# The four links of a head's norm get places of their own in an iteration of the attention loop

## The chip, the cores and the metric

One NeuronCore of a Trainium2 chip runs the whole program. The metric is the device time of one execution in microseconds (us). An execution is also recorded by the hardware profiler; its rows are quoted below. Engines: PE is TensorE (PEld its weight loads), DVE is VectorE, ACT is ScalarE, POOL is GpSimd, SP issues DMAs.

## The reference, cut to what matters

The program is two blocks of two layers each, on 256 positions of width 1024. The first block's layers hold the attention that the change touches. A layer of it attends with 4 heads; a head has two softmax maps, whose difference weighs the values, and each head's output is normalized over its 128 channels:

```python
def diff_attn(q, k, v, lam):
    s = jnp.einsum('bhqd,bhkd->bhqk', q, k).astype(jnp.float32) * (HEAD_DIM ** -0.5)
    a = jax.nn.softmax(s, axis=-1).reshape(b, N_HEADS, 2, nq, nk)
    w = a[:, :, 0] - lam * a[:, :, 1]
    return jnp.einsum('bhqk,bhkd->bhqd', w.astype(v.dtype), v)

def head_out(o, g_sub, lam_init):
    o = rms_norm(o, g_sub) * (1.0 - lam_init)
    b, h, n, d = o.shape
    return o.transpose(0, 2, 1, 3).reshape(b, n, h * d)
```

The 256 positions of `x` attend to 512 keys (256 of the context, 256 of their own). In the first layer the 256 context positions also attend, to their own 256 keys. Beside attention, a layer pools (`pool_mixer`), projects with `w_out` and runs an MLP; `ada_params` gives its shifts, scales and gates from `c @ w_ada`.

## The kernel before

Everything runs in float32. A weight matrix arrives in pieces of 512 rows (`raw`), is split into a high part (`whi`, ScalarE, L111) and the rest (`wlo`, VectorE, L119), and every product takes three passes: high by high, high by low, low by high. `Stream` holds this pipeline; a product takes a unit of weights at a time, and its `tick` and `next` put the splits of later units between the matmuls. Most matmuls are issued at L593.

Each engine runs its instructions in the order in which the program issues them, so the order of the lines is the schedule. Work that is to lie beside other work is written as generators, whose `next` runs one more piece: `fill(i)` gives `FILL[l][i]` pieces of the layer's other products (values' projection `v_gemm`, pooling's projection `u_gemm` with its windows L933 to L951, pooling's product L958 to L967, the first half of `w_out`), and `st.ada_step()` gives `STEPS[l][i]` pieces of the next layers' `ada_params`, whose weights come as `araw` (sums on VectorE at L278 and L280, or products on TensorE at L293, with a copy at L296, transposes at L301 and a sum at L303).

`attend` (L973) runs the attention of one layer. Its items are, for `x`, a head's first and second 128 queries (8 items), and in the first layer a context head's 256 queries (4 more). The loop has two iterations more than items. In iteration i:

- `scores(i + 1)` puts the next item's products on TensorE (L987);
- `soft(i)` runs its first piece: maxima (DVE, L997), their scaling (L998) and the exponentials (ACT, L1002);
- `before`, the third piece of `soft(i-1)`, is the weighted difference of the two maps (DVE, L1012);
- `fill(i)`;
- the second piece of `soft(i)`: reciprocal and scaling of the sums (DVE, L1006 and L1007), scaling of the second map (ACT, L1009);
- the adaLN steps;
- the rest of the norm of a head whose values were begun one iteration ago: the product with `ones` (PE, L1037), Ln and Exp (ACT, L1039 and L1040), the scaled output (DVE, L1041), and `split`, its high part (ACT, L445) and the rest (DVE, L446);
- `flip(i - 1)`: transposes of the weighted maps (PE, L1024) and their copy `wT` (ACT, L1025);
- two iterations after a head's last item, `values` begins: the products with the values (PE, L1033) and the squares of the result (ACT, L1035).

There are 12 heads in all: 4 of `x` and 4 of the context in the first layer, 4 of `x` in the second. In the first layer the heads of `x` begin in iterations 3, 5, 7 and 9, those of the context in 10 to 13; in the second layer the heads begin in iterations 3, 5, 7 and 9. The last head of each layer ends behind the loop.

Of the kernel before, what the change touches and what calls it, by code (L numbers as in the profile page):

```python
# [71 lines left out]
class Stream:  # L72
# [90 lines left out]
    def next(self, hold=False):  # L163
        u = self.cur
        self.cur += 1
        self.held = self.held + 1 if hold else 1
        self.split_to(self.cur)
        if self.HI_AT < 0:
            self.high_to(self.room())
        self.due += self.quota[u]  # L170
        return self.parts.pop(u)
# [8 lines left out]
def _body(es, tc, I, out, dbg, stop):  # L180
    nc = tc.nc
    mm, act, dve, pool_e, pe = nc.tensor.matmul, nc.scalar, nc.vector, nc.gpsimd, nc.tensor
# [8 lines left out]
    def bank(shape=(128, 2, T)):  # L191
        return ps.tile(list(shape), F32, tag="ps", bufs=8, name="ps")

    def scr(shape, tag="s", bufs=5, dt=F32):
        return (mp if tag in SMALL else sp).tile(list(shape), dt, tag=tag, bufs=bufs, name=tag)

    def scr1(shape=(128, T)):
        return scr(shape, tag="s1", bufs=6)
# [14 lines left out]
    def w4(name, shape):  # L213
        return sp.tile(list(shape), F32, tag="w4", bufs=2, name=name)
# [229 lines left out]
    def split(src, hi, lo, lo_eng=None):  # L444
        act.copy(hi, src)  # L445
        (lo_eng or dve).tensor_sub(lo, src, hi)  # L446
# [242 lines left out]
    def run(g):  # L689
        for _ in g:  # L690
            pass
# [135 lines left out]
    for k in range(8):  # L827
# [3 lines left out]
        for a in range(0, 0 if k in DIRECT else 4, 2):  # L831
            hi = wp.tile([128, 2, 512], F32R, tag="whi", bufs=Stream.BUFS, name="whi")
            lo = wp.tile([128, 2, 512], F32R, tag="wlo", bufs=Stream.BUFS, name="wlo")
# [26 lines left out]
    h = {}  # L860
# [112 lines left out]
    def attend(l, segs, qT, kT, v, operand, look, fill):  # L973

        items = [(s, h, qts) for s in segs for h in range(4) for qts in (((0,), (1,)) if s == 0 else ((0, 1),))]
        keys_of = {0: (0, 1, 2, 3), 1: (2, 3)}
        sc, wts, wT = {}, {}, {}

        def scores(i):
            if i >= len(items):  # L980
                return
            s, h, qts = items[i]
            nk, k0 = 128 * len(keys_of[s]), 128 * keys_of[s][0]
            sc[i] = [bank([128, len(qts), nk]) for _ in range(2)]
            for a, qt in enumerate(qts):
                for j in range(2):
                    mm(sc[i][j][:, a], qT[64 * j:64 * j + 64, h, s * T + qt * 128:s * T + qt * 128 + 128],  # L987
                       kT[64 * j:64 * j + 64, h, k0:k0 + nk], start=True, stop=True)

        def soft(i):  # L990
            s, _, qts = items[i]
            nq, nk = len(qts), 128 * len(keys_of[s])
            m = scr([128, 2, 2], tag="m2", bufs=3)[:, :, :nq]
            z = scr([128, 2, 2], tag="z2", bufs=3)[:, :, :nq]
            banks, e = sc.pop(i), []
            for j in range(2):
                dve.reduce_max(m[:, j], banks[j], axis=AX)  # L997
            dve.tensor_scalar(m, m, -0.125, None, op0=OP.mult)  # L998
            for j in range(2):
                ei = scr([128, nq, nk])  # L1000
                for a in range(nq):
                    act.activation(ei[:, a], banks[j][:, a], AF.Exp, bias=m[:, j, a:a + 1], scale=0.125,  # L1002
                                   accum_out=z[:, j, a:a + 1])
                e.append(ei)
            yield
            dve.reciprocal(z, z)  # L1006
            dve.tensor_mul(z[:, 1], z[:, 1], lam[l].to_broadcast([128, nq]))  # L1007
            for a in range(nq):
                act.activation(e[1][:, a], e[1][:, a], AF.Copy, scale=z[:, 1, a:a + 1])  # L1009
            yield  # L1010
            for a in range(nq):
                dve.scalar_tensor_tensor(e[0][:, a], e[0][:, a], z[:, 0, a:a + 1], e[1][:, a], op0=OP.mult, op1=OP.add)  # L1012
            wts[i] = e[0]

        def flip(i):
            s, h, qts = items[i]
            n = len(keys_of[s])
            w = wts.pop(i)
            if qts[0] == 0:
                wT[s, h] = w4("wT", [128, 4, T])  # L1020
            p = bank([128, n, len(qts), 128])
            for a in range(len(qts)):
                for j in range(n):
                    pe.transpose(p[:, j, a], w[:, a, j * 128:(j + 1) * 128], ident)  # L1024
            act.copy(wT[s, h][:, :n, qts[0] * 128:(qts[-1] + 1) * 128].rearrange("p n (a t) -> p n a t", t=128), p)  # L1025

        def values(s, h):
            t, keys = wT.pop((s, h)), keys_of[s]
            hi, lo = operand(s)
            b = bank()  # L1030
            p, p2 = b[:, 0], b[:, 1]
            for i, kt in enumerate(keys):
                mm(p, v[:, kt, h * 128:(h + 1) * 128], t[:, i], start=i == 0, stop=i == len(keys) - 1)  # L1033
            o = scr1()
            act.activation(o, p, AF.Square)  # L1035
            yield
            mm(p2, ones, o, start=True, stop=True)  # L1037
            r = scr1()
            act.activation(r, p2, AF.Ln, bias=eps, scale=1.0 / 128)  # L1039
            act.activation(r, r, AF.Exp, scale=-0.5)  # L1040
            dve.scalar_tensor_tensor(o, p, gsub[:, l:l + 1], r, op0=OP.mult, op1=OP.mult)  # L1041
            split(o, hi[:, 4 + h], lo[:, 4 + h])

        for i in range(look):
            scores(i)
        vals = None
        before = iter(())
        last = {(s, h): max(i for i, x in enumerate(items) if x[:2] == (s, h)) for s, h, _ in items}
        for i in range(len(items) + 2):
            scores(i + look)  # L1050
            now = soft(i) if i < len(items) else iter(())
            next(now, None)
            next(before, None)
            fill(i)
            next(now, None)
            for _ in range(STEPS[l][i]):
                st.ada_step()
            before = now
            if vals is not None:
                next(vals, None)  # L1060
                vals = None
            if 1 <= i <= len(items):
                flip(i - 1)
            for sh, at in last.items():
                if i == at + 2:
                    vals = values(*sh)
                    next(vals)
        if vals is not None:
            next(vals, None)

    def hooked(g, at, f):

# [108 lines left out]
    def first_layer(l, norm, h):  # L1181
# [155 lines left out]
        if l == 0:  # L1337
            small_setup()
        attend(l, segs, qT, kT, v, operand, 1, fill)
        mark("w_out")  # L1340
        st.ahead = st.BUFS
# [707 lines left out]
```

## Time and profile before

| | |
|---|---|
| time, median of 3 runs | 1658.03 us (1655.99 to 1660.52) |
| time of the profiled execution | 1653.65 us |
| its span in the profile | 1651.9 us |
| TensorE busy | 1571.6 us (95%) |
| VectorE busy | 1221.6 us (74%) |
| ScalarE busy | 862.8 us (52%) |
| GpSimd busy | 82.5 us (5%) |
| mean granted TensorE clock | 0.97 |

The profile's times are microseconds from the span's start. The attention loop of the first layer lies at about 105 to 237, that of the second at about 695 to 769. A row of the trace's order of time gives the start, the duration, the engine, the line, the operation, what it writes and reads, shapes, a count where like rows are merged, and in brackets the idle time of the engine before it with what ended it.

### The profile page before, as it was taken

How to read it: one execution, taken by the hardware profiler on the slowest of the kernel's cores; microseconds unless marked ns; L12 is line 12 of the kernel's file. 1: busy time of each engine (PE TensorE's matmuls, PEld its weight loads, DVE VectorE, ACT ScalarE, POOL GpSimd, SP SyncE). 2: the span in 40 equal slices, each digit the busy share in tenths (PEclk: the TensorE clock that was granted, in tenths of full speed). 3: DMA queues.
4: the chain of work that ended last, by engine and by line, in shares of the span. 5: the costliest groups of instructions: out<-in, count | busy, mean ns of one | idle time of the engine just before them, and what ended most of it. 6: DMA issues, size and time to landing. Idle time of an engine off the chain costs nothing.

```text
span 1651.9 us, 31245 instructions
## 1 busy us (share of the span) xinstructions
PE 1571.6 (95%) x12917; PEld 1475.2 (89%) x12917; DVE 1221.6 (74%) x2105; ACT 862.8 (52%) x1471; POOL 82.5 (5%) x202
## 2 busy tenths in 40 slices
PE   7899798999999999798999999989999999899998
PEld 2886488999999999777999998669999998899998
DVE  6885478899978777656856677568886788897673
ACT  5646356522222225765744457436664558766463
POOL 0010000112121120000000000000000000000000
PEclk9999999999999999998999999779999999999999
DMA  9353323355455553212656554115655544555551
GB/s 367 121 153 106 122 90 118 128 179 180 155 202 192 192 180 109 77 52 90 211 179 202 179 179 129 52 58 175 203 180 180 198 153 159 179 178 185 178 197 55
DMA packets 134014, 256.89 MB, mean 156 GB/s; under 512 B 6224, under 2 KB 19184, under 8 KB 132848
## 3 DMA queue, kind: packets, MB, share of 16 engines
q1 hardware_dynamic: 132672, 254.31, 46.4%
q8 instruction: 101, 1.65, 0.4%
q10 hardware_dynamic: 1200, 0.59, 0.1%
q14 instruction: 41, 0.34, 0.1%
HBM read 253.83 MB, written 1.05 MB: 154 GB/s over the span
## 4 chain that ended last, share of the span: by engine, by line
PE 81%; DVE 8%; ACT 8%; issue 2%; DMA 1%; SPq 0%; DVEq 0%; ACTq 0%
PE ps L593 73%; DVE wlo L119 2%; ACT whi L111 1%; PE ps L987 1%; ACT s L922 1%; ACT s L524 1%; PE ps L293 1%; PE ps L1033 1%; ACT s L1002 1%; DMA raw<-in_w_ada_dram 1%; DVE s L942 1%; PE ps L1610 1%; DVE X L714 0%; PE ps L1024 0%; PE ps L1684 0%
## 5 line engine op out<-in xcount | busy, mean ns | idle before, releaser
L111 ACT CAST whi<-raw 128x1024 fp32r<-128x1024 f32 x380 | 394.2, 1048 | 427.5 <-PE ps L593 392.1
L119 DVE TENSOR_TENSOR wlo<-raw,whi 128x1024 fp32r<-128x1024 f32 x380 | 459.1, 1221 | 160.9 <-ACT whi L111 155.9
L593 PE MATMUL ps<-hid,whi 128*128 128x256 f32 x2304 | 295.5, 283 | 0.0
L593 PEld LDWEIGHTS ps<-hid,whi 128*128 128x128 f32 x2304 | 284.8, 192 | 0.0
L593 PE MATMUL ps<-h2hi,whi 128*128 128x256 f32 x672 | 162.2, 283 | 4.9 <-ACT h2hi L525 4.9
L593 PE MATMUL ps<-h2lo,whi 128*128 128x256 f32 x672 | 161.9, 281 | 0.0
L593 PE MATMUL ps<-hid,wlo 128*128 128x256 f32 x1152 | 156.8, 283 | 0.0
L593 PE MATMUL ps<-fhi,whi 128*128 128x256 f32 x640 | 155.3, 281 | 0.0
L593 PE MATMUL ps<-flo,whi 128*128 128x256 f32 x640 | 155.3, 281 | 0.0
L280 DVE SCALAR_TENSOR_TENSOR aacc<-araw,cs,aacc 128x512 f32<-128x512 f32 x182 | 129.1, 747 | 25.5 <-DMA araw<-in_w_ada_dram 24.6
L593 PEld LDWEIGHTS ps<-hid,wlo 128*128 128x128 f32 x1152 | 146.4, 192 | 0.0
L593 PEld LDWEIGHTS ps<-h2hi,whi 128*128 128x128 f32 x672 | 128.1, 191 | 5.3 <-ACT h2hi L525 5.3
L593 PEld LDWEIGHTS ps<-h2lo,whi 128*128 128x128 f32 x672 | 127.5, 190 | 0.3 <-DVE h2lo L527 0.3
L593 PE MATMUL ps<-dhi,whi 128*128 128x256 f32 (+1 forms) x512 | 126.5, 285 | 0.0
L593 PE MATMUL ps<-dlo,whi 128*128 128x256 f32 (+1 forms) x512 | 124.9, 281 | 0.0
L593 PEld LDWEIGHTS ps<-fhi,whi 128*128 128x128 f32 x640 | 121.1, 189 | 0.0
L593 PEld LDWEIGHTS ps<-flo,whi 128*128 128x128 f32 x640 | 120.5, 188 | 0.0
L593 PEld LDWEIGHTS ps<-dhi,whi 128*128 128x128 f32 x512 | 96.9, 189 | 0.5 <-issue 0.3
L593 PEld LDWEIGHTS ps<-dlo,whi 128*128 128x128 f32 x512 | 97.0, 189 | 0.2
L714 DVE SCALAR_TENSOR_TENSOR X<-ps,ada,X 128x256 f32<-128x256 f32 x184 | 75.9, 476 | 20.1 <-PE ps L593 20.1
L593 PE MATMUL ps<-fhi,wlo 128*128 128x256 f32 x640 | 89.3, 282 | 0.0
L593 PE MATMUL ps<-h2hi,wlo 128*128 128x256 f32 x672 | 88.8, 281 | 0.0
(392 smaller groups left out, 2820.4 us busy)
## 6 DMA issues: line engine op xcount, KB each, us to landing
raw<-in_w_mlp_dram SPq DMA_DIRECT2D x64, 1024.0 KB, 5.5
raw<-in_ffn_w_up_dram SPq DMA_DIRECT2D x48, 1024.0 KB, 5.1
araw<-in_w_ada_dram SPq DMA_DIRECT2D x80, 512.0 KB, 4.0
raw<-in_ffn_w_down_dram SPq DMA_DIRECT2D x24, 1024.0 KB, 5.3
raw<-in_w_in_dram SPq DMA_DIRECT2D x16, 1024.0 KB, 5.6
raw<-in_ev_w_in_dram SPq DMA_DIRECT2D x12, 1024.0 KB, 5.0
raw<-in_w_out_dram SPq DMA_DIRECT2D x8, 1024.0 KB, 4.8
raw<-in_od_w_in_dram SPq DMA_DIRECT2D x8, 1024.0 KB
```

The lines of the kernel that those rows point to most:

```text
L111: self.nc.scalar.copy(hi, src)
L119: self.nc.vector.tensor_sub(lo, src, hi)
L280: dve.scalar_tensor_tensor(a[:, v], raw[:, k], c, a[:, v], op0=OP.mult, op1=OP.add)
L293: mm(p[:2], cs[:, :, 2 * q + k], raw[:, k], start=q == 0 and k == 0, stop=q == 3 and k == 1)
L524: act.activation(h, src, AF.Identity, bias=sa(n), scale=gs(n))
L593: mm(p, w, x, start=start, stop=stop, skip_group_check=True)
L714: dve.scalar_tensor_tensor(X[:, n, s], b[:, i], gates[s](n), X[:, n, s], op0=OP.mult, op1=OP.add)
L922: act.copy(sw[32 * q:32 * q + 32], src[32 * (q ^ 1):32 * (q ^ 1) + 32])
L942: dve.tensor_add(c[:, :, :width], a[:, :, :width], a[:, :, n:n + width])
L987: mm(sc[i][j][:, a], qT[64 * j:64 * j + 64, h, s * T + qt * 128:s * T + qt * 128 + 128], kT[64 * j:64 * j + 64, h, k0:k0 + nk], start=True ...
L1002: act.activation(ei[:, a], banks[j][:, a], AF.Exp, bias=m[:, j, a:a + 1], scale=0.125, accum_out=z[:, j, a:a + 1])
L1033: mm(p, v[:, kt, h * 128:(h + 1) * 128], t[:, i], start=i == 0, stop=i == len(keys) - 1)
```

## The change

The norm of a head now runs in five pieces instead of two, and the loop calls them at places of their own. `values` gets three more `yield`s, and `split` is written out as its two operations. In the loop, `vals` is the head that was begun in the iteration before, and `old` the head before that. At the top of an iteration, ahead of the next scores, comes the product with `ones`. Behind the second piece of `soft(i)` come Ln and Exp. Behind the adaLN steps come the scaled output and its high part. The rest (the low part) comes in the iteration after that, behind the third piece of `soft(i-1)` and ahead of `fill`. Behind the loop, `run` ends what is left of the last two heads.

```diff
@@ values
             mm(p2, ones, o, start=True, stop=True)
+            yield
             r = scr1()
             act.activation(r, p2, AF.Ln, bias=eps, scale=1.0 / 128)
             act.activation(r, r, AF.Exp, scale=-0.5)
+            yield
             dve.scalar_tensor_tensor(o, p, gsub[:, l:l + 1], r, op0=OP.mult, op1=OP.mult)
-            split(o, hi[:, 4 + h], lo[:, 4 + h])
+            act.copy(hi[:, 4 + h], o)
+            yield
+            dve.tensor_sub(lo[:, 4 + h], o, hi[:, 4 + h])
@@ the loop
-        vals = None
-        before = iter(())
+        vals = old = before = iter(())
         last = {(s, h): max(i for i, x in enumerate(items) if x[:2] == (s, h)) for s, h, _ in items}
         for i in range(len(items) + 2):
+            next(vals, None)
             scores(i + look)
             now = soft(i) if i < len(items) else iter(())
             next(now, None)
             next(before, None)
+            next(old, None)
             fill(i)
             next(now, None)
+            next(vals, None)
             for _ in range(STEPS[l][i]):
                 st.ada_step()
             before = now
-            if vals is not None:
-                next(vals, None)
-                vals = None
+            next(vals, None)
+            old, vals = vals, iter(())
             if 1 <= i <= len(items):
                 flip(i - 1)
             for sh, at in last.items():
                 if i == at + 2:
                     vals = values(*sh)
                     next(vals)
-        if vals is not None:
-            next(vals, None)
+        run(old)
+        run(vals)
```

## Rows read from the trace of the kernel before

**Rows 1.** The page: busy time by engine, and the chain that ended last.
```profile
PE 1571.6 (95%) x12917; PEld 1475.2 (89%) x12917; DVE 1221.6 (74%) x2105; ACT 862.8 (52%) x1471; POOL 82.5 (5%) x202
...
PE 81%; DVE 8%; ACT 8%; issue 2%; DMA 1%; SPq 0%; DVEq 0%; ACTq 0%
```
**Rows 2.** Busy time in two stretches: length, each engine, clock, DMA share, GB/s.
```profile
136.00:237.00 101.00, 88.39 (x494) 61.70 (x494) 53.31 (x123) 52.28 (x133) 0.00 (x0) 0.95 0.31 101
714.00:769.00 55.00, 45.00 (x281) 38.22 (x281) 30.88 (x80) 29.83 (x73) 0.00 (x0) 0.88 0.19 63
```
**Rows 3.** Line 1041, VectorE's idle time before it: releaser, us in total, times.
```profile
  ACT s L1040: 28.4, 10
```
**Rows 4.** Order of time, TensorE, first layer: its waits in the loop.
```profile
174.46 1.88 PE L293 MATMUL ps<-araw,cs 128*2 128x512 f32 x4 [2.13 <-DMA araw<-in_w_ada_dram]
...
187.25 2.23 PE L293 MATMUL ps<-araw,cs 128*2 128x512 f32 x3 [2.03 <-DVE ada L303]
...
204.88 0.58 PE L301 MATMUL ps<-ident,arow 2*128 2x2 f32 x4 [3.48 <-ACT arow L296]
...
213.85 0.38 PE L593 MATMUL ps<-mhi,whi 128*128 128x256 f32 x1 [1.64 <-ACT mhi L964]
...
236.45 0.70 PE L1037 MATMUL ps<-s,ones 128*128 128x256 f32 x2 [1.39 <-ACT s L1035]
```
**Rows 5.** Order of time, TensorE, second layer: values of two heads, and waits.
```profile
730.64 1.89 PE L1033 MATMUL ps<-wT,v 128*128 128x256 f32 x8
...
746.19 1.11 PE L1024 MATMUL ps<-ident,s 128*128 128x128 f32 x4 [4.88 <-DVE s L1012]
747.10 3.62 PE L1033 MATMUL ps<-wT,v 128*128 128x256 f32 x8
752.13 0.70 PE L958 MATMUL ps<-uT,wpool 128*128 128x256 f32 x2 [1.42 <-ACT uT L951]
756.03 1.22 PE L958 MATMUL ps<-uT,wpool 128*128 128x256 f32 x2 [3.19 <-ACT uT L951]
...
768.05 0.70 PE L1037 MATMUL ps<-s,ones 128*128 128x256 f32 x2 [0.47 <-ACT s L1035]
```
**Rows 6.** Order of time, TensorE, first layer: the values of three heads.
```profile
134.32 1.89 PE L1033 MATMUL ps<-wT,v 128*128 128x256 f32 x8
...
196.63 1.89 PE L1033 MATMUL ps<-wT,v 128*128 128x256 f32 x8
...
219.73 1.03 PE L1033 MATMUL ps<-wT,v 128*128 128x256 f32 x4
```
**Rows 7.** Order of time, ScalarE, first layer: the squares of the same heads.
```profile
137.81 0.39 ACT L1035 ACTIVATE s<-ps 128x256 f32<-128x256 f32 x1
...
200.75 0.38 ACT L1035 ACTIVATE s<-ps 128x256 f32<-128x256 f32 x1
...
225.65 0.39 ACT L1035 ACTIVATE s<-ps 128x256 f32<-128x256 f32 x1
```
**Rows 8.** Order of time, second layer: scaling of head 1, squares of heads 2 and 3.
```profile
723.88 0.48 DVE L1041 SCALAR_TENSOR_TENSOR s<-ps,gsub,s 128x256 f32<-128x256 f32 x1 [5.43 <-ACT s L1040]
...
737.43 0.40 ACT L1035 ACTIVATE s<-ps 128x256 f32<-128x256 f32 x1
...
759.20 0.39 ACT L1035 ACTIVATE s<-ps 128x256 f32<-128x256 f32 x1
```
**Rows 9.** Order of time, VectorE and ScalarE: the norm of the first context head.
```profile
224.35 0.48 DVE L1041 SCALAR_TENSOR_TENSOR s<-ps,gsub,s 128x256 f32<-128x256 f32 x1
225.30 0.43 DVE L446 TENSOR_TENSOR mlo<-s,mhi 128x256 fp32r<-128x256 f32 x1 [0.47 <-ACT mhi L445]
...
224.86 0.41 ACT L445 CAST mhi<-s 128x256 fp32r<-128x256 f32 x1 [3.69 <-DVE s L1041]
225.17 0.58 ACT L1025 COPY wT<-ps 128x512 f32<-128x512 f32 x1
```
**Rows 10.** Busy time in a stretch behind the 4.88 wait (columns as in rows 2).
```profile
746.00:748.00 2.00, 1.81 (x7) 1.63 (x8) 1.34 (x3) 2.00 (x6) 0.00 (x0) 0.50 0.00 0
```

## The prediction

> **What bounds the kernel now.** I read the page first: TensorE is busy 95% of the span and carries 81% of the chain that ended last [rows 1]. So a change can only matter where TensorE stands. The table of stretches comes next. It gives the two attention loops, from the values of the first head to the last product with `ones`: in the first layer's 101.0 us TensorE worked 88.4, in the second layer's 55.0 it worked 45.0, at a mean clock of 0.95 and 0.88 [rows 2]. About 22 us are idle there, and the change moves only work of these loops. Behind them TensorE is dense again, so what it loses or gains here goes into the end one to one.
>
> The line that the change splits shows why one would split it: VectorE stood idle 28.4 us in 10 waits before L1041, the product of a head's values with its norm, for ScalarE's Exp of L1040 [rows 3]. That is idle time of an engine that is mostly not the bound. So I read TensorE's own waits last. In the first layer: two for the adaLN weights `araw` (the first is 2.13 us), 2.03 on L303, 3.48 on the copy L296, 1.64 on L964 and 1.39 on the last Square [rows 4]. In the second: 4.88 on the softmax sum L1012, then 1.42 and 3.19 on the pooling's L951, and 0.47 on the last Square [rows 5].
>
> **The change part by part.** No instruction is added or taken away: 12 heads keep their Square, product with `ones`, Ln, Exp, scaling, copy and difference. Only places in the three engines' orders change, and no DMA moves. Four moves count.
>
> 1. *The product with `ones` goes from the end of the next iteration to its very top*, ahead of the scores and of all of `fill`. It needs the Square (L1035), which ScalarE runs at the end of the iteration before, behind all that iteration's copies. Until now one iteration of TensorE's work lay between. Now TensorE's order is values, product with `ones`, scores, fill, and all of it waits for ScalarE. The price of one wait: where ScalarE is free it is 0.47, the last head's wait today, whose product follows its values directly [rows 5]. Where ScalarE is behind it is the Square's end less the values' end. In the trace:
>    - first head, first layer: values end 134.32+1.89 = 136.21, Square ends 137.81+0.39 = 138.20: 2.0 [rows 6, 7].
>    - fourth head: values end 198.52, Square 201.13: 2.6 [rows 6, 7].
>    - second context head: values end 220.76, Square 226.04: 5.3 [rows 6, 7].
>    - second layer, second head: values end 732.53, Square 737.83: 5.3; third head: 750.72 and 759.59: 8.9 [rows 5, 8].
>    - the other heads: about 0.5.
>
> 2. *Ln and Exp go behind the softmax's own scaling, ahead of the adaLN steps.* They no longer wait for the fill. ScalarE then holds 0.9 more ahead of the copy L296 in one iteration.
>
> 3. *The scaling (L1041) and the copy of the high part keep their place behind the adaLN steps.* So in the context heads the order on ScalarE stays: the high copy waits for L1041 on VectorE, which stands behind the sums of L280 (ScalarE waits 3.69 there), then the flip's copy L1025, then the Square [rows 9]. This is why the Square of the second context head stays late; nothing in the change pulls it forward.
>
> 4. *The difference (the low part, L446) goes into the iteration after.* Today VectorE waits 0.47 for the copy and works 0.43 ahead of the next softmax maximum [rows 9]. That 0.9 leaves the chain from a head's norm to the next softmax.
>
> Now the sum, as a balance of TensorE's idle time, since its work is the same. I leave the two waits for `araw` out on both sides: TensorE's own reading frees that buffer, so they move with it.
>
> *First layer.* Idle now 2.03+3.48+1.64+1.39 = 8.5. After: the first head waits 2.0 (nothing ahead of it changes). Second and third 0.5 each, so TensorE reaches the eighth iteration about 2.5 late (2.0+0.5), and the softmax chain, which starts from the third head's values there, too. From then on ScalarE gains the 0.9 of move 4 and runs 1.6 late. The wait on L303 becomes 1.6 (TensorE 0.4 later still, by the third head's own wait). Fourth head: 2.6-2.5+1.6 = 1.7. The copy L296 comes 2.5 late (1.6 and the 0.9 of move 2), TensorE 4.7 late (2.5, 1.7, and the product itself): 3.48 becomes 1.2. First context head: I take 1.6, an estimate, since the 0.9 of move 2 and the high copy put its Square 1.4 late and TensorE has caught up to 0.3; 0.5 is the low end. L964: 0, as TensorE arrives later than it. Second context head: Square 0.4 late, TensorE 0.6 late: 5.1. The last two: 0.5 each. Together 2.0+0.5+0.5+1.6+1.7+1.2+1.6+5.1+0.5+0.5 = 15.2, less 8.5: **+6.7**.
>
> *Second layer.* The first head waits 0.6. Today VectorE stands 5.43 before its L1041 [rows 8], since TensorE's fill lies ahead of the product with `ones`; now Ln and Exp follow ScalarE's L1009 and the wait falls under 2. With the 0.9 of move 4 the next maxima come some 4.6 earlier, but the exponentials stand behind the flip's copy and come 2.2 earlier (an estimate), and so does the pooling's chain behind them. The second head's wait is 5.3-2.2-0.6 = 2.5. The flip that waited 4.88 then waits for nothing, since the softmax sum is ready about 3 earlier (2.2 and the 0.9) and TensorE comes about 2 later. TensorE so ends the third head's values near 747.0, 3.7 earlier than today. But its Square stands behind two rounds of the pooling's windows and comes only 2.7 earlier, at 756.9: TensorE waits 9.9, and the waits of 1.42 and 3.19 vanish inside that. Balance: 0.6+2.5+9.9 = 13.0, against 4.88+1.42+3.19 = 9.5: +3.5.
>
> The clock takes part of that back. Behind the 4.88 idle TensorE is granted 0.50 [rows 10], and ran so from 746.19 to 750.7; it did again after the 3.19. These are the low of its two levels, 1.2 GHz for 2.4. About 9.7 us of work at half speed lose 4.8. With one long idle in place of two, one such stretch of 5 us remains: 2.4 lost, so -2.4. **Second layer +1.1.** In the first layer a slow stretch after the 3.48 idle goes and one after the new 5.1 comes, which I put at 0.
>
> Beside that stands a rule of the Trainium skill (TensorE: Matmul & The Clock Gate, section What's actually happening): the halved clock is the default, and activity releases it. By it the 5.1 us wait alone would be followed by a slow stretch like that after the 4.88, costing about 2.3 more, and the sum would be 10.1 in place of 7.8; the trace agrees on the kind of effect, with 0.50 after 4.88 us of idle.
>
> Sum: 6.7+1.1 = **+7.8 us**. The profiled execution took 1653.65 (span 1651.9 and 1.75 around it), so it would take 1661.5. The median of the runs shown is 1658.03, 4.4 above the profiled one; on that basis the forecast is **1665.8**, 0.47% slower.
>
> Bounds. Low: the second context head's Square comes directly behind its values (5.1 becomes 0.5) and the second layer gains 3 instead of losing 1.1 (its long idle stretches shrink with the pooling chain): 7.8-4.6-4.1, about -1. High: nothing comes earlier than today: the waits are 2.6, 5.3 (less 0.6 for TensorE's own delay) and 8.9, L296 still costs 3.48, and the slow stretch comes: about +17.
>
> **The rivals.**
> *Faster.* The chain through L1041 leaves the softmax's path (28.4 us of VectorE's idle [rows 3]) and the new waits are all at their floor. Then 9.5 of idle and 4.8 of slow clock go in the second layer and 7.1 in the first (2.03, 3.48, 1.64), of which about 2 remain in each; ten floors of 0.5 cost 5.0: -12.4, that is 1645.6. It decides at one point: that the Square ends within 0.5 us of its head's values, so that ScalarE has nothing queued. The 2.0, 2.6, 5.3, 5.3 and 8.9 above speak against it; for it, that five heads are at the floor already. By a rule of the Trainium skill (Perfetto Trace Analysis, section Optimizing Scalar/DVE Operations: where Scalar and Vector aren't saturated but cause bubbles on other engines, breaking their work up may let it end sooner) this would be the outcome; ScalarE is busy 52% and VectorE 74% on the page, so its condition holds, but the link that TensorE waits for, the Square, isn't made earlier.
> *No difference.* The new waits take the place of old idle time in the first layer too. This is so if the Square of the second context head isn't held by the adaLN sums, which would need VectorE to have run them in the time that it no longer stands before L1041: 7.8-4.6 = +3.2, or 1661.2. Against it: they stand ahead of L1041 in VectorE's order before and after, and one waits for its load.
> *Slower still.* The waits fall at today's full sizes, +12 to +17, or up to 1675.
>
> **How the numbers follow.** About 0.3%, 5 us, is what a measurement of this kernel tells from no change. The forecast (+5 to +12) has a chance of 0.63, slower still 0.07, no difference 0.20, faster 0.10. So slower 0.70, same 0.20, faster 0.10. The range takes the bounds: from 1657 (-1) to 1675 (+17); below it lie the faster rival and a part of no difference.
>
> **What would show it.** In the changed profile TensorE's idle before L1037 on ACT L1035 grows from 1.39+0.47 to some 24 us in eight or more waits, the longest two at the second layer's third head (9 to 10) and the first layer's second context head (5). VectorE's 28.4 before the scaling falls below half. The 4.88 before the flip is gone, and so are 1.64 and 1.42. The first loop is 5 to 8 us longer, the second 0 to 3. It is wrong if the waits on the Square sum to under 12 us, or if the first loop isn't longer.

## The result, and the profile after

The changed kernel is slower: 1669.02 us (median of 5) against 1657.81, a ratio of 1.0085 with a 95% interval from 1.0071 to 1.0100 (the two medians alone stand at 1.0068). On another chip, beside the last three experiments below, the same kernel stood at 1.0069 (1.0053 to 1.0085); one of its six runs there took 1918.22 us at a mean granted clock of 0.742, where the others had 0.967 to 0.974, and is not in that ratio. So the loss is 9 to 17 us; +7.8 had been forecast.

The page of the changed kernel, busy time by engine and the chain that ended last, tells nothing yet. The engines do the same work as in [rows 1], to within 2 us each; only the span is 1666.9 in place of 1651.9.

```profile
PE 1572.4 (94%) x12917; PEld 1476.8 (89%) x12917; DVE 1221.4 (73%) x2105; ACT 863.5 (52%) x1471; POOL 82.5 (5%) x202
...
PE 81%; ACT 8%; DVE 7%; issue 2%; DMA 1%; SPq 0%; DVEq 0%; ACTq 0%
```

The table of stretches of the changed kernel, with the same columns as [rows 2], shows the place. Each stretch runs, as there, from about the end of the first head's values to the last product with `ones`:

```profile
137.00:247.00 110.00, 87.28 (x496) 61.11 (x497) 52.57 (x123) 52.40 (x134) 0.00 (x0) 0.95 0.29 93
725.00:781.00 56.00, 42.33 (x280) 36.41 (x279) 31.15 (x81) 30.31 (x73) 0.00 (x0) 0.91 0.21 70
```

The first loop takes 110.0 in place of 101.0, and TensorE works no more in it (87.3 and 88.4). The second takes 56.0 in place of 55.0. From here on a loop is measured from the start of the first head's values to the start of the second matmul of the last product with `ones` (each such product is two in the trace). So measured they grow from 102.45 to 111.35 and from 56.19 to 57.06: +8.9 and +0.9.

Where TensorE stands now is told by its order of time, here its waits for the Square (in brackets; line 1037 is still the product with `ones`):

```profile
138.96 0.70 PE L1037 MATMUL ps<-s,ones 128*128 128x256 f32 x2 [2.04 <-ACT s L1035]
...
204.16 0.70 PE L1037 MATMUL ps<-s,ones 128*128 128x256 f32 x2 [3.13 <-ACT s L1035]
...
208.66 0.41 PE L301 MATMUL ps<-ident,arow 2*128 2x2 f32 x4 [0.93 <-ACT arow L296]
...
211.72 0.70 PE L1037 MATMUL ps<-s,ones 128*128 128x256 f32 x2 [1.21 <-ACT s L1035]
...
227.54 1.22 PE L1037 MATMUL ps<-s,ones 128*128 128x256 f32 x2 [7.17 <-ACT s L1035]
...
238.36 0.70 PE L1037 MATMUL ps<-s,ones 128*128 128x256 f32 x2 [0.47 <-ACT s L1035]
...
747.17 0.70 PE L1037 MATMUL ps<-s,ones 128*128 128x256 f32 x2 [2.39 <-ACT s L1035]
...
768.46 1.22 PE L1037 MATMUL ps<-s,ones 128*128 128x256 f32 x2 [10.20 <-DVE s L1012]
```

The row at 238.36 stands for four waits of 0.47 in the first loop; the second has one of 0.62 and one of 0.47 besides. Together TensorE stands 15.4 us in the first loop and 13.7 in the second before this product. In the kernel before it stood 1.39 and 0.47 [rows 4, 5]. (The last row names L1012, which ends at 768.43; the Square of that head ends at 768.41, as the rows below show, and the wait of this product's weight load is put down to the Square.) The old waits of 4.88, 1.42, 3.19 and 1.64 are gone, and 3.48 has become 0.93.

Why 7.17: VectorE and ScalarE in the stretch ahead of it.

```profile
220.81 2.73 DVE L280 SCALAR_TENSOR_TENSOR aacc<-araw,cs,aacc 128x512 f32<-128x512 f32 x4
224.47 1.42 DVE L280 SCALAR_TENSOR_TENSOR aacc<-araw,cs,aacc 128x512 f32<-128x512 f32 x2 [0.93 <-DMA araw<-in_w_ada_dram]
225.80 0.48 DVE L1043 SCALAR_TENSOR_TENSOR s<-ps,gsub,s 128x256 f32<-128x256 f32 x1
...
226.31 0.41 ACT L1044 CAST mhi<-s 128x256 fp32r<-128x256 f32 x1 [3.67 <-DVE s L1043]
226.63 0.58 ACT L1025 COPY wT<-ps 128x512 f32<-128x512 f32 x1
227.10 0.39 ACT L1035 ACTIVATE s<-ps 128x256 f32<-128x256 f32 x1
...
768.02 0.39 ACT L1035 ACTIVATE s<-ps 128x256 f32<-128x256 f32 x1
768.46 0.50 PEld L1037 LDWEIGHTS ps<-s,ones 128*128 128x128 f32 x2 [10.60 <-ACT s L1035]
```

The scaling (now L1043) stands behind six adaLN sums; the high copy on ScalarE waits 3.67 for it, then come the flip's copy and the Square. TensorE's values had ended at 220.37. It is the order of [rows 9], 1.5 us later, of which 0.7 is the loop's later start; what was no wait of TensorE then is one now, as its next matmul is the one that needs this Square.

### The profile page after: what moved, and what is told of

Its sections match the earlier page's. It is cut to its first block, busy times and chain, and to the rows that moved or that the text cites. A ratio compares the mean times of both kernels' runs of the same rounds, so it can differ in the third digit from the quotient of the medians.

```text
span 1666.9 us, 31243 instructions
## 1 busy us (share of the span) xinstructions
PE 1572.4 (94%) x12917; PEld 1476.8 (89%) x12917; DVE 1221.4 (73%) x2105; ACT 863.5 (52%) x1471; POOL 82.5 (5%) x202
## 4 chain that ended last, share of the span: by engine, by line
PE 81%; ACT 8%; DVE 7%; issue 2%; DMA 1%; SPq 0%; DVEq 0%; ACTq 0%
PE ps L593 73%; DVE wlo L119 2%; ACT whi L111 1%; PE ps L987 1%; ACT s L922 1%; ACT s L524 1%; ACT s L1002 1%; DVE s L942 1%; DMA raw<-in_w_ada_dram 1%; PE ps L293 1%; PE ps L1615 1%; PE ps L1037 0%; DMA araw<-in_w_ada_dram 0%; PE ps L1033 0%; DVE X L714 0%
```

## The experiments

The theory: the product with `ones` at the top of the iteration holds scores and fill, which follow it in TensorE's order, until ScalarE comes to the Square. (In the trace no matmul starts inside the wait of 7.17; the next ones start at 228.20, behind the product.) Rivals: the other moves (Ln and Exp, the low part) lose the time; or a part of the loss is not in the loops at all. All ratios are against the kernel before on the same chip; a us of difference is 0.06%.

**One link put back.** Of the change, only the product with `ones` goes behind the fill:

```diff
-            next(vals, None)
             scores(i + look)
 ...
             fill(i)
+            next(vals, None)
```

> The change with one of its links moved: the product with ones stands behind the iteration's fill, ahead of the second softmax piece, in place of the top of the iteration; the other links stay where the change put them. Theory (TensorE's wait for the Square at the top of the iteration is the loss): the waits on the Square, 26 us in the changed kernel, fall to under 4, the 7.2 and 10.2 us waits are gone, and the time is 1653 to 1659, at or a little under the kernel before. Rival 1 (the loss comes from the other moves: Ln and Exp behind the softmax's own scaling, the low part an iteration later): the time stays at 1664 or more with few waits on the Square. Rival 2 (part of the loss lies outside the loops and belongs to the changed program): the loops are back, but 1661 to 1664 remain.

Measured: 1652.81 us, 0.9991 (0.9980 to 1.0002), 0.2 us under the expected range. The whole loss is gone. What ended TensorE's idle time before line 1037 (us, count; TensorE's two queues are counted, so a wait stands in it about twice) is 5.7, where the changed kernel has 52.9 and one more of 10.2:

```profile
  ACT s L1035: 5.7, 6
```

In its order of time the wait of 4.88 before the second layer's flip is 2.83:

```profile
741.46 0.66 PE L1024 MATMUL ps<-ident,s 128*128 128x128 f32 x4 [2.83 <-DVE s L1012]
```

The other three links in their new places cost nothing that can be measured. In this one profile the loops are 99.8 and 53.7, shorter than the 102.5 and 56.2 before; the time doesn't tell it from no change.

**That link alone.** The kernel before, with the product with `ones` at the top and the rest of the norm together, as before (a `yield` behind the product parts them):

```diff
 ...
+            yield
 ...
         for i in range(len(items) + 2):
+            if vals is not None:
+                next(vals)
             scores(i + look)
```

> The kernel before with one link moved: the product with ones at the top of the iteration; Ln, Exp, the scaling and both parts stay together behind the adaLN steps, as before. Theory (the place of this product is the loss): 1667 to 1674, at or above the changed kernel, with waits on the Square of 2.0, about 3, 7 and 10 us; a little worse than the change, as it keeps the low part ahead of the next maximum. Rival 1 (the other moves lose it): 1655 to 1660.

Measured: 1673.33 us, 1.0108 (1.0095 to 1.0122). The one move makes the whole loss, and by the loops (117.3 and 57.4) some more. With the one before, the theory holds against both rivals.

**The low part alone.**

```diff
             next(before, None)
+            next(old, None)
             fill(i)
 ...
```

> The kernel before with one link moved: the low part of a head's output goes into the next iteration, behind the weighted difference of the softmax. Theory: 0.9 us leaves the chain from a head's norm to the next maximum, where that chain sets TensorE's waits, three or four times: 0 to 4 us faster than before, 1653 to 1658; the wait of 4.9 before the second layer's flip falls to about 4. Rival 1 (the low part in its new place holds VectorE's fill work): 1659 or more.

Measured: 1654.15 us, 0.9995 (0.9985 to 1.0005): no difference, in the range that either no gain or the small one would give. The trace shows the sought effect, a flip that waits 3.16 where it waited 4.88:

```profile
742.78 1.11 PE L1024 MATMUL ps<-ident,s 128*128 128x128 f32 x4 [3.16 <-DVE s L1012]
```

**The scaling ahead of the adaLN steps.** In the change, this should bring the late Square forward:

```diff
             next(vals, None)
+            next(vals, None)
             for _ in range(STEPS[l][i]):
                 st.ada_step()
             before = now
-            next(vals, None)
```

> The change with the scaling and the high part ahead of the adaLN steps, all other links as the change has them. Theory (the Square of the second context head is late because the high part ahead of it on ScalarE waits for the scaling, which stands behind the adaLN sums on VectorE): its wait falls from 7.2 to 1 us or less, the slow stretch of TensorE behind it is gone, and the time is 6 to 9 us under the change: 1660 to 1663. Rival (the Square is late for another reason, or the sums then come later and hold the same chain elsewhere): within 2 us of the change, 1667 to 1671.

Measured: 1670.03 us, 1.0087 (1.0072 to 1.0102): the rival. Two waits of TensorE, and VectorE ahead of the first of them:

```profile
194.27 5.70 PE L293 MATMUL ps<-araw,cs 128*2 128x512 f32 x8 [4.43 <-DVE s L1043]
...
228.34 0.70 PE L1037 MATMUL ps<-s,ones 128*128 128x256 f32 x2 [4.04 <-ACT s L1035]
...
193.73 0.48 DVE L1043 SCALAR_TENSOR_TENSOR s<-ps,gsub,s 128x256 f32<-128x256 f32 x1 [1.84 <-ACT s L1041]
194.13 0.15 DVE L303 TENSOR_TENSOR ada<-ps,pv 128x8 f32<-128x8 f32 x1
```

The cause was right in kind, but the wait of 7.17 falls to 4.04 and not to 1 or less. Ahead of the Square ScalarE still waits 2.18 for the softmax's L1007, which stands behind two adaLN sums of the fill on VectorE; then come L1009, Ln, Exp and the high copy:

```profile
223.12 1.41 DVE L280 SCALAR_TENSOR_TENSOR aacc<-araw,cs,aacc 128x512 f32<-128x512 f32 x2
...
224.85 0.91 ACT L1009 ACTIVATE s<-s,z 128x256 f32<-128x256 f32 x2 [2.18 <-DVE z L1007]
```

In the eighth iteration the adaLN sum L303 now stands behind the scaling, which waits 1.84 for Exp. TensorE's adaLN products, which waited 2.0 to 2.2 for L303 [rows 4], now wait 4.43, and the trace puts that down to the scaling. So one wait was traded in part for another. The waits together fell all the same: TensorE is idle 19.3 us in this first loop, where the change has 22.8 and, in its second profile, 21.3. The loop is no shorter (111.6), as TensorE's work in it takes 92.4 us in place of 88.6 and 90.8, at a mean granted clock of 0.92. Whether the move itself lowers the clock isn't shown.

**Two heads at the top, and ten.** Which waits make the loss: the two long ones or the many short ones?

```diff
+            at_top = (l, i) in ((0, 12), (1, 8))
+            if at_top:
+                next(vals, None)
             scores(i + look)
 ...
             fill(i)
+            if not at_top:
+                next(vals, None)
```

> The change with the product with ones at the top of the iteration for two heads alone (the second context head of the first layer, the third head of the second layer), and behind the fill for the other ten, where TensorE doesn't wait for the Square. Theory (these two waits are most of the loss, because the Square stands behind VectorE's adaLN sums there and behind the pooling's windows here): 8 to 13 us over the version with all products behind the fill, 1661 to 1666; first loop 105 to 108, second 57 to 59. Rival (the many short waits, which delay the whole chain from the first head on, are most of it): 1654 to 1658.

Measured: 1663.06 us, 1.0046 (1.0033 to 1.0060); loops of 107.2 and 57.5, with these two waits:

```profile
223.88 1.22 PE L1037 MATMUL ps<-s,ones 128*128 128x256 f32 x2 [6.81 <-ACT s L1035]
...
762.93 1.22 PE L1037 MATMUL ps<-s,ones 128*128 128x256 f32 x2 [9.43 <-DVE s L1012]
```

The reverse (`not in`):

> The reverse: the product with ones at the top for ten heads, behind the fill for those two. Theory (the two long waits are most of the loss): 1654 to 1659; first loop 101 to 103, second 54 to 56; the waits of 2.0, 3.1 and 2.4 us for the Square stay. Rival (the many short waits are most of it): 1661 to 1666.

Measured: 1660.06 us, 1.0027 (1.0016 to 1.0038), between the two expected ranges; loops of 109.4 and 53.3. Against the version with all products behind the fill (99.8 and 53.7), the second loop is clear: its third head's wait is its whole loss. In the first loop the lengths alone mislead: 7.4 more for the one head, 9.6 more for the others, and 11.6 for the change, which has both. The stretches tell why (columns as in [rows 2]; all behind the fill, then the one head, then the others at the top):

```profile
134.13:233.92 99.79, 88.20 (x501) 60.91 (x500) 54.28 (x128) 52.16 (x133) 0.00 (x0) 0.97 0.33 105
134.83:242.04 107.21, 88.78 (x501) 61.70 (x500) 54.27 (x128) 52.36 (x133) 0.00 (x0) 0.95 0.31 99
135.13:244.53 109.40, 92.13 (x501) 62.67 (x500) 54.35 (x128) 51.94 (x133) 0.00 (x0) 0.94 0.31 97
```

TensorE's idle time, the length less its work, is 11.6, 18.4 and 17.3: 6.8 more for the one head and 5.7 for the others, against 11.2 and 9.7 in the two profiles of the change. So the waits nearly add up, and the other 3.9 of the 9.6 is TensorE's same work taking longer, at a mean granted clock of 0.94 in place of 0.97. The times add up as well: 0.55% and 0.36% over the version with all products behind the fill, 0.94% or, on the other chip, 0.78% for the change.

With the long wait taken out, two shorter ones come instead, one of 1.48 behind the fill for the same head, and one of 2.16 at the top of the next iteration for the head after it:

```profile
230.78 0.48 PE L1037 MATMUL ps<-s,ones 128*128 128x256 f32 x1 [1.48 <-ACT s L1035]
...
234.94 0.68 PE L1037 MATMUL ps<-s,ones 128*128 128x256 f32 x1 [2.16 <-ACT s L1035]
```

So the two long waits are somewhat more than half of the loss: all of it in the second layer, about half of it in the first.

**Amid the fill.** A try at a better kernel: half of the fill's pieces ahead of the product with `ones`, half behind it.

```diff
-            fill(i)
+            fill(i, vals)
 ...
+            n = FILL[l][i]
+            for k in range(n):
+                if k == (n + 1) // 2:
+                    next(head, None)
                 next(filler, None)
+            if n < 2:
+                next(head, None)
```

> The change with the product with ones in the middle of the iteration's fill: half of the fill's pieces lie between a head's values and this product, and half between it and Ln. Theory: the wait for the Square is hidden by the first half in most heads, and Ln no longer waits for the whole fill: the two longest waits fall by half or more, 1650 to 1656, at best 2 us under the version with the product behind the fill. Rival (the Square comes later than half a fill in the two late heads, and their waits stay at 3 us or more): 1656 to 1662.

Measured: 1659.99 us, 1.0026 (1.0016 to 1.0036), in the rival's range. Half a fill hides the Square of most heads, but not that of the second context head:

```profile
223.04 0.48 PE L1037 MATMUL ps<-s,ones 128*128 128x256 f32 x1 [4.31 <-ACT s L1035]
```

That this wait makes the longer time isn't shown: the loops of this profile, 103.0 and 54.7, are no longer than those of the kernel before (102.5 and 56.2). Where its 4 us lie stays open.

**The clock behind the long waits.** In the changed kernel the 48 matmuls behind the wait of 7.17 took 8.38 us, at a mean granted clock of 0.69. To price that alone, TensorE was kept at work during the two longest waits with products that nothing reads:

```diff
+            n = {(0, 12): 40, (1, 8): 56}.get((l, i), 0)
+            if n:
+                d = bank([128, 128])
+                for _ in range(n):
+                    mm(d, ident, ident, start=True, stop=True)
             next(vals, None)
```

> The change, with products of the identity by itself that nothing reads, 40 ahead of the product with ones of the second context head and 56 ahead of that of the second layer's third head: TensorE works through its two longest waits (7.2 and 10.2 us). They end inside the waits (about 0.15 us each, 5.9 and 8.2 us), so no wait ends later. Theory (the slow stretch that follows a long idle costs what my sum left out, 3 us in the first layer and some 2.4 in the second): the granted clock stays 1.0 behind both, the 48 matmuls after the first take 6.0 in place of 8.4, and the time is 4 to 6 us under the change, 1662 to 1666. Rival (the slow stretch costs nothing, since another engine sets the end of what follows): within 1.5 us of the change, 1667 to 1671.

Measured: 1671.83 us, 1.0103 (1.0086 to 1.0120), just above the rival's range. I had put such a product at 0.15 us and it took 0.22, so they ran past the Square's end, by 1.6 and 2.2 us, and took back a part, or all, of what the clock gave. For the first of the two, the products and the Square:

```profile
221.05 9.09 PE L1057 MATMUL ps<-ident 128*128 128x128 f32 x80
229.98 0.60 PE L1037 MATMUL ps<-s,ones 128*128 128x256 f32 x2
...
228.03 0.39 ACT L1035 ACTIVATE s<-ps 128x256 f32<-128x256 f32 x1
```

The loops are 111.7 and 57.0, as in the change. They come from the fastest of its six runs (1663.97 us), and the change itself wasn't run on this chip; so what the products did to the time stays open. With 28 and 40 of them:

> As the kernel that works through the two longest waits, with 28 and 40 products of the identity in place of 40 and 56, since one took 0.224 us there and they ran 2.4 and 2.2 us beyond the waits: 6.3 and 9.0 us, inside waits of 7.2 and 10.2. Theory (the slow stretch behind the two waits costs 3 and about 2.4 us): the product with ones starts as early as in the change, the 48 matmuls behind it take 6.0 in place of 8.4, the first loop is 108 to 109 and the second 54.5 to 55.5, and the time is 4 to 6 us under the change on the same chip. Rival (what follows is set by another engine, so that the clock costs nothing): the loops stay at 111 and 57 and the time within 1.5 us of the change.

Measured: 1666.90 us, 1.0075 (1.0063 to 1.0087), where the change itself has 1.0069 (1.0053 to 1.0085) on this chip: no difference in the time, where 4 to 6 us less had been expected. The trace does tell the price inside the loop. First the stretch of the 48 matmuls in the changed kernel, then in this one (columns as in [rows 2]), and last this one's order of time, with its products of the identity and the wait that remains:

```profile
228.20:236.58 8.38, 8.38 (x52) 8.29 (x51) 5.14 (x8) 1.52 (x4) 0.00 (x0) 0.69 0.55 170
```

```profile
227.98:234.00 6.02, 6.02 (x52) 5.99 (x51) 5.45 (x9) 1.74 (x4) 0.00 (x0) 1.00 0.36 101
```

```profile
220.30 6.42 PE L1057 MATMUL ps<-ident 128*128 128x128 f32 x56
227.64 0.70 PE L1037 MATMUL ps<-s,ones 128*128 128x256 f32 x2 [0.93 <-ACT s L1035]
```

Same matmuls, 6.02 in place of 8.38, and 0.70 in place of 1.22 for the product ahead of them: about 2.9 us lost to the slow clock behind the 7.17 wait. The wait ends where it did. The first loop is 108.6 in place of 111.4. In the second the stretch behind the wait is 2.1 shorter, but 1.5 of it went to a slow stretch ahead of it (at 745.8 to 749.2), which made the values of the third head and its Square 1.5 later; the loop is 56.5, where 54.5 to 55.5 had been expected. Why the gain in the loops doesn't show in the time stays open.

**Both kernels once more**, for the part outside the loops, which the first two profiles show 5.2 us longer after the change.

> The change itself, for its size on the same chip as the other experiments and a second profile. Theory (the change costs 9 to 13 us in the two loops, the rest of its measured 14 is where slow stretches of the clock fall outside them): ratio 1.006 to 1.009; the loops again 110 to 112 and 56 to 59; the stretches outside differ from the first profile's by up to 3 us. Rival (the change costs a fixed 5 us outside the loops): the stretches outside are again 5 us longer than in the profile of before.

> The kernel before once more, for a second profile. Theory: the stretches outside the loops differ from the first profile's by up to 3 us, with the slow clock in them; the loops are 99 to 103 and 53 to 56. Rival (the stretches outside are the program's own, and the change lengthens them): they agree with the first profile's within 0.5 us.

Measured: the change 1667.15 us, 1.0069, loops of 112.1 and 57.2, within 0.1 of what was expected; the kernel before 1657.74 us in its one run, loops of 104.2 and 56.3, both a little over the expected range. Outside the loops the change now takes 1488.8 where its first profile had 1498.5, a difference of 9.7 in place of the expected 3 at most; the kernel before takes 1495.4 and 1493.2. The largest part is the stretch from the last head's product with `ones` to the end, here in the two profiles of the change and then the two of before:

```profile
780.40:1666.90 886.50, 857.62 (x7580) 829.53 (x7580) 647.69 (x1041) 512.59 (x798) 1.91 (x2) 0.97 0.48 161
```

```profile
778.90:1658.10 879.20, 852.91 (x7580) 826.50 (x7578) 647.35 (x1041) 512.15 (x798) 1.91 (x2) 0.98 0.49 163
```

```profile
768.00:1651.90 883.90, 856.18 (x7580) 828.35 (x7580) 647.52 (x1041) 512.29 (x798) 1.91 (x2) 0.97 0.49 162
```

```profile
772.30:1656.00 883.70, 855.64 (x7580) 827.96 (x7578) 647.34 (x1041) 512.37 (x798) 1.91 (x2) 0.97 0.50 162
```

The same program takes 886.5 and 879.2 here, and the kernel before lies between. The stretches at half clock in it sum to 54 and 40 us of the two, and to 51 in both of before; the half of the 14 us between 54 and 40 is close to the 7.3 by which the change's two profiles differ. So the fixed 5 us of the rival are not there, and this part isn't shown to be a cost of the change. In the loops the mean of two profiles gives 159.6 before and 168.9 after: +9.3.

## Why the prediction was right in its direction, and which term was small

The mechanism was right. Step 1, that the product with `ones` at the top makes TensorE wait for a Square that ScalarE reaches late, is shown by putting that one link back (0.9991) and by moving it alone (1.0108). The two longest waits are at the two heads named, and the balance of idle time holds nearly term by term:

- first head 2.0 forecast, 2.04 measured; second and third 0.5 and 0.47; the last two likewise;
- L296 1.2 and 0.93; first context head 1.6 and 1.21; L964 0 and none;
- L303 1.6 and 2.19 (2.18 in the second profile);
- fourth head 1.7, and 3.13 in the first profile, 1.55 in the second;
- second context head 5.1 and 7.17 (7.28 in the second profile);
- second layer: 0.6, 2.5 and 9.9 forecast, 0.62, 2.39 and 10.20 measured. Its loop: +1.1 forecast, +0.9 measured.

The term that was mis-sized is the first layer's idle time, +6.7. Its loop in the two profiles of before and then the two of the change (columns as in [rows 2]):

```profile
134.32:236.77 102.45, 89.83 (x501) 62.84 (x500) 54.86 (x128) 52.28 (x133) 0.00 (x0) 0.95 0.31 100
134.25:238.45 104.20, 91.42 (x501) 62.55 (x500) 54.84 (x128) 52.38 (x133) 0.00 (x0) 0.93 0.32 98
135.03:246.38 111.35, 88.55 (x501) 61.85 (x500) 54.40 (x128) 52.19 (x133) 0.00 (x0) 0.95 0.30 95
133.76:245.84 112.08, 90.82 (x501) 62.10 (x500) 54.35 (x128) 52.13 (x133) 0.00 (x0) 0.94 0.30 94
```

TensorE is idle 12.6 and 12.8 before, 22.8 and 21.3 after: +10.2 in the first pair and +8.5 in the second. Its work takes 1.3 and 0.6 less, where I had put the clock at 0. So the clock term was near, and the idle term 2 to 3.5 too small, most of it at the second context head. For that head I had TensorE 0.6 late and the Square 0.4 late. Counted from the first head's values, its own values end at 86.4 before and 85.3 after in the first pair (86.7 and 86.8 in the second), and the Square at 91.7 and 92.5 (93.5 and 94.0). So TensorE wasn't late, and the Square was 0.7 and 0.5 late. The size that I started from was also one execution's: between the values and the Square lie 5.3 us in the first profile of before, and 6.8 in the second.

The slow stretches did move as forecast, and they cancel only in the sum. Ahead of this wait TensorE ran 10.2 us at half clock before and none after (13.7 and 6.8 in the second pair); the time so won went into the longer wait. Behind it came a slow stretch, which costs 2.9, as the experiment that kept TensorE at work shows. The prediction named 10.1 as its sum by the rule of the Trainium skill (TensorE: Matmul & The Clock Gate, section What's actually happening) that the halved clock is the default and activity releases it. The slow stretch behind the wait is there (0.69 over 8.38 us), but TensorE's work in the whole loop took no longer by it. So that 10.1 comes nearer to the loops' +9.3 than 7.8 does is luck.

What remains between the loops' +9.3 and the 11.2 of the medians is within what the stretches outside the loops vary from one execution to the next. For that reason the step that what is lost or gained in the loops goes into the end one to one isn't shown at the size of a few us: in the version with the product behind the fill and in the one with the low part alone late, the loops are 5 to 7.5 us shorter than in the kernel before, and the times stand at 0.9991 and 0.9995.

Of the signs, the waits on the Square came to 29.1 us in twelve where some 24 in eight or more were named, and the first loop grew by 8.9 and 7.9, at the upper end of the 5 to 8 or above it. One sign was wrong: VectorE's wait of 28.4 before the scaling was to fall below half. It is 24.3 in the changed kernel, with 2.5 on another releaser. Two of its waits, 6.29 and 6.27, are at the last two context heads, whose products with `ones` now come late (at 238.36 and 246.06):

```profile
240.10 0.48 DVE L1043 SCALAR_TENSOR_TENSOR s<-ps,gsub,s 128x256 f32<-128x256 f32 x1 [6.29 <-ACT s L1041]
```

The sign measured an engine that isn't the bound.

Of the rivals, "faster" had its condition, a Square within 0.5 us of the values, and five heads met it (0.47), one came near it (0.62), and the others did not. "No difference" needed the adaLN sums out of the way; the experiment that put the scaling ahead of them shows that the wait does fall (7.17 to 4.04), and that another wait on VectorE grows (2.19 to 4.43).

No version beats the kernel before by what can be measured. The change with the product behind the fill comes nearest, at 0.9991.

## What to carry to other kernels

Splitting a chain into links is safe on the engine that waits for them least, and dangerous on the bound one: before moving a matmul up, look up where in the queue of the engine that feeds it its input stands, and what that queue waits for. Put it behind enough work that doesn't need it; the top of the next iteration is the place with the least. When the balance of waits is made, keep TensorE's idle time and its work apart, in more than one profile of each kernel: a slow stretch behind a wait lengthens the loop (2.9 us here), and one ahead of it can shorten the wait (as at the second context head) or, where the engine that ends the wait needs TensorE's results, move its end too (1.5 us in the second loop of the kernel with 28 and 40 products).

## What the runs showed of the hardware that was not expected

A single-core program of 1650 us varied by up to 7 us over an unchanged stretch of 880 us (886.5 and 879.2) with the share of it at half clock (54 and 40 us), so one pair of profiles can't price a change of 10 us by its spans; the two loops by themselves tell it (111.4 and 112.1 against 102.5 and 104.2). Over all thirteen profiles the span less the two loops runs from 1488.8 to 1498.7, and the changed kernel alone takes almost all of that range (1488.8 and 1498.5). A float32 product of 128x128 by 128x128 took about 0.22 us back to back at full clock (forty of them began at 221.05 and the next product at 229.98: 8.93 by 40).
